# One transformer layer on one core: seven-product blocks for two more projections, cross weights folded elsewhere, pools laid out anew

## The chip, the cores and the metric

The kernel runs on one core of a Trainium2 chip. A core has TensorE for matrix products (PE in the profile; PEld is its loading of the stationary operand), VectorE (DVE), ScalarE (ACT) and GpSimd (POOL) for elementwise work, and a sync engine (SP) whose queue issues this kernel's DMAs. Matrix products go to PSUM, in banks of 128 x 512 floats; all other tiles are in SBUF. The metric is the device time of the whole program in microseconds, as the median of several runs.

## What is computed

One layer of a streaming encoder on 2048 tokens of width 1024, all in float32. Cut to what matters:

```
u = rms_norm(h, g_mix_pre)
z = u @ w_in                                   # 1024 x 2816
qa, ka, va, qh, fh, ih, gh = split(z)          # 512,128,128,512,512,512,512
ya = swa_with_sinks(qa, ka, va, sinks)         # 8 heads of 64, window of 128 tokens
yh = hgrn2(qh, fh, ih, gh, lb, onorm)          # gated recurrence, 4 heads of 128
y  = concat([ya, yh]) @ w_out                  # 1024 x 1024
h  = h + rms_norm(y, g_mix_post)
u  = rms_norm(h, g_x_pre)
m  = rms_norm(mem, g_mem)                      # 256 memory tokens
h  = h + rms_norm(cross_attention(u, m, wq, wk, wv, wo), g_x_post)
u  = rms_norm(h, g_ffn_pre)
h  = h + rms_norm((silu(u @ w_gate) * (u @ w_up)) @ w_down, g_ffn_post)   # inner 2816
```

## The kernel before

Every float32 product is made of three: each operand is split into a rounded part hi and the remainder lo, and hi*hi, hi*lo and lo*hi are summed in PSUM. `mm3` issues these for the projections, `products` for the later stages. The kernel is written as Python generators; a scheduler of the language then puts the instructions of each engine in an order, by the order in which they were written and by what is ready, so work written later can move forward into gaps if its buffers are free.

**The stages.** (1) `mix` normalises the tokens (`norm_half`, with transposes in `transpose_split`) and multiplies them with 22 column tiles of `w_in`, for the first 1024 tokens (b=0) and then for the second (b=1). `wcols` (L141) loads and splits a column tile; `in_cols` runs 24 matmuls for each half of 512 tokens, applies the gates (`decays` makes the recurrence's cumulative factors), and stores z to memory. (2) Beside the first 13 column groups, `fold_cross` multiplies the fixed memory tokens into the cross-attention weights (qk_d and vo_d). (3) `swa` and `hgrn` run attention and recurrence for 16 tiles of 128 tokens, between the column tiles; the last eight steps of the recurrence have nothing written beside them but the loading of `w_out`. (4) `out_proj` makes 16 rows of the output projection, 48 matmuls each, then the norm (`post_norm`), the residual, and the transposed result h1t_d. (5) `phases` runs the rest, scores, values, hidden layer and down projection, in blocks of 256 x 1024 x 1024.

**The blocks.** A block is either of kind "s", seven products of half-size operands (`seven`, a Strassen-like scheme; 84 matmuls of 512 columns for 1024 deep) or of kind "p", the usual eight (`eight`; 96 matmuls). The operand that stays for many blocks ("resident") is held as tiles T, numbered 1 to 8: 1, 8, 2, 3 are its quarters, 5, 7, 6, 4 are sums and differences, built by `resident` from raw halves. "p" needs 1, 2, 8, 3; "s" needs 1, 5, 6, 3, 7, 2, 4. There are seven slots, four of kind A in pool `big`, three of kind B in pool `tb`. The other operand is streamed: `streamed` loads raw tiles (three buffers) and makes S tiles (five buffers) by `split2`, which rounds hi on ACT ("A") or POOL ("P") and subtracts for lo on VectorE. Products accumulate in banks g and t (two each); h and s serve transposes and the small work. `after` of a block (norms, stores, transposes) is run beside the next block. At a change of the resident, the last block and the first are of kind "p", so that fewer tiles are needed while slots change hands.

**Space.** `mix` and `out_proj` hold pools `wp` (weight columns) and `io` (rows) on the right side of SBUF through both; pools xp, ap and later tb lie on the left. So the output projection may begin while the recurrence still runs.

Of the kernel before, what the change touches and what calls it, by code (L numbers as in the profile page):

```python
# [26 lines left out]
NB = 2  # L27
# [13 lines left out]
class Layer:  # L41
# [15 lines left out]
    def xr_tile(self):  # L57
        self._n += 1
        return self.ph.tile([P, D], F32, tag="xr", name=f"xr_{self._n}", bufs=2)

# [52 lines left out]
    def post_norm(self, banks, g, res, dst, t):  # L113
        nc = self.nc
        ss = self.small("p_s", 2)
        for q in range(2):
            nc.scalar.activation(t[:, q * 512:(q + 1) * 512], banks[q], AF.Square, accum_out=ss[:, q:q + 1])
        r = self.rstd([ss[:, 0:1], ss[:, 1:2]], D, "p")
        for q in range(2):
            sl = slice(q * 512, (q + 1) * 512)  # L120
            nc.vector.scalar_tensor_tensor(t[:, sl], banks[q], r, g[:, sl], ALU.mult, ALU.mult)
        nc.gpsimd.tensor_tensor(t, t, res, ALU.add)
        self.store(dst, t)

# [33 lines left out]
    def mm3_pair(self, banks, pairs):  # L158

        nc = self.nc  # L160
        n = len(pairs)
        for i, ((ah, al), (bh, bl)) in enumerate(pairs):
            for q in range(2):
                sl = slice(q * 512, (q + 1) * 512)
                nc.tensor.matmul(banks[q], ah, bh[:, sl], start=(i == 0), stop=False)
                nc.tensor.matmul(banks[q], ah, bl[:, sl], start=False, stop=False)
                nc.tensor.matmul(banks[q], al, bh[:, sl], start=False, stop=(i == n - 1))


    def run(self):  # L170
# [5 lines left out]
        self.y_d = tc.dram_tile([NT, P, KT, P], F32, name="y_d")  # L176
# [9 lines left out]
        with (  # L186
            tc.tile_pool(name="cst", bufs=1) as self.cst,
            tc.tile_pool(name="sm", bufs=3, **kw) as self.sm,
            tc.tile_pool(name="ps", bufs=2, space=PS, **kw) as self.psum,
        ):  # L190
            self.consts()
            with (
                tc.tile_pool(name="gp", bufs=2, **kw) as self.gp,
                tc.tile_pool(name="big", bufs=4, **kw) as self.big,
                contextlib.ExitStack() as self.wp_io,
            ):
                self.wp = self.wp_io.enter_context(tc.tile_pool(name="wp", bufs=3, side="right", **kw))
                self.io = self.wp_io.enter_context(tc.tile_pool(name="io", bufs=2, side="right", **kw))
                wt = self.mix()
                with tc.tile_pool(name="tb", bufs=3, **kw) as self.tb:  # L200
                    self.rows(wt)

    def mix(self):
        tc, I = self.tc, self.I
        kw = dict(reuse_waits="tile")
        us = [[] for _ in range(NB)]
        wt = []

        def norm(b, s, xs=None):
            xs = xs or self.norm_loads(I["x"], b, s, "xxxx" if b else "xxxs")  # L210
            hi, lo = [self.big.tile([P, KT, 512], F32R, tag="big", name=f"u{i}{b}_{s}") for i in "hl"]
            self.norm_half(xs, self.g_mix, us[b], hi, lo, "sh")

        def nxt(b, s):
            if b + 1 < NB:
                norm(b + 1, s)
            else:
                self.out_weights(s, wt)

        with tc.tile_pool(name="mc", bufs=1, **kw) as self.mc:  # L220
            with tc.tile_pool(name="xp", bufs=1, **kw) as self.ph:
                self.g_mix = self.gain(I["g_mix_pre"])
                xs = self.norm_loads(I["x"], 0, 0, "xxxs")
                norm(0, 0, xs)
                norm(0, 1)
                self.mix_consts()
                cols = self.in_proj(0, us[0], lambda: nxt(0, 0))
                side = self.fold_cross()
                for i in range(13):
                    next(cols)  # L230
                    for _ in range(2 if i % 3 else 4):
                        next(side, None)
                for _ in side:
                    pass
            with tc.tile_pool(name="ap", bufs=1, **kw) as self.ph:
# [3 lines left out]
                next(swa)  # L239
                for _ in cols:  # L240
                    pass
                nxt(0, 1)
                cols = self.in_proj(1, us[1], lambda: nxt(1, 0))
                for _ in swa:
                    next(hgrn)
                for _ in hgrn:
                    pass
                for i in range(5):
                    next(cols)
# [5 lines left out]
                nxt(1, 1)  # L255
                for _ in self.hgrn(range(NPB, NT), "hs"):
                    pass
        return wt
# [9 lines left out]
    def fold_cross(self):  # L268

        nc, ph = self.nc, self.ph  # L270
# [5 lines left out]
        kT = [ph.tile([P, KT, M], F32R, name=f"kT{i}") for i in range(2)]  # L276
        vT = [ph.tile([P, KT, M], F32R, name=f"vT{i}") for i in range(2)]

        def split_tiles():
            self._n += 1  # L280
            return [ph.tile([P, D], F32R, tag=t, name=f"{t}_{self._n}", bufs=2) for t in ("xh", "xl")]

        for t in range(M // P):
            m = self.xr_tile()
# [4 lines left out]
        for w, dst in ((self.I["wk_x"], kT), (self.I["wv_x"], vT)):  # L289
            for j in range(KT):  # L290
                raw = self.xr_tile()
                self.load(raw.rearrange("p (k c) -> p k c", k=KT),
                          w[:, j * P:(j + 1) * P].rearrange("(k p) c -> p k c", p=P))
                wh, wl = split_tiles()
                self.split(raw, wh, wl)
                ps = self.bank("sh"[j % 2])[:, :M]
                self.mm3(ps, [((wh[:, k * P:(k + 1) * P], wl[:, k * P:(k + 1) * P]), (mT[0][:, k, :], mT[1][:, k, :]))
                              for k in range(KT)])
                nc.scalar.activation(dst[0][:, j, :], ps, AF.Copy)
                nc.vector.tensor_tensor(dst[1][:, j, :], ps, f32(dst[0][:, j, :]), ALU.subtract)  # L300
                yield
        for d in range(KT):
            wq = self.xr_tile()
# [15 lines left out]
            yield  # L319
        for h in range(4):  # L320
            banks = [[self.bank(k) for k in "sh"] for _ in range(2)]
            for i in range(2):
                j = 2 * h + i
                raw = self.xr_tile()
# [21 lines left out]
    def mix_consts(self):  # L346
# [24 lines left out]
        self.wmask = ph.tile([P, M], F32, name="wmask")  # L371
# [3 lines left out]

        self.reset = ph.tile([P, 8, 64], F32, name="reset")
        nc.vector.memset(self.reset, 1.0)
        nc.vector.memset(self.reset[:, :, 0:1], 0.0)
# [7 lines left out]

        self.dl = ph.tile([P, 4, T // 64 + 1], F32, name="dl")
        nc.vector.memset(self.dl[:, :, 0:1], 0.0)
        self.G = ph.tile([P, NT, 4, 2], F32, name="G")
        self.G1 = ph.tile([P, NT, 4], F32, name="G1")  # L390

    def zero_tiles(self):
        nc, ph = self.nc, self.ph
# [10 lines left out]
    def norm_loads(self, src, b, s, tiles="xxxx"):  # L404

        xs = []
        for t in range(4):
            x = self.xr_tile() if tiles[t] == "s" else self.io_tile("x")
            r0 = b * TB + s * 512 + t * P
            self.load(x, src[r0:r0 + P, :])  # L410
            xs.append(x)
        return xs

    def norm_half(self, xs, g, u, hi, lo, kinds):

        for t, x in enumerate(xs):
            n = self.pre_norm(x, g, True)
            o = t * P
            self.transpose_split(n, lambda q: hi[:, 4 * q:4 * q + 4, o:o + P],
                                 lambda q: lo[:, 4 * q:4 * q + 4, o:o + P], kinds)  # L420
        u.append((hi, lo))

    def in_proj(self, b, u, mid):
        order = [4, 5, 0, 1, 2, 3]
        for h in range(4):
            order += [10 + h, 6 + h]
        order += range(14, 22)
        e1 = None
        for cols in [order[:2]] + [[c] for c in order[2:-2]]:
            e1 = self.in_cols(b, u, cols, e1)  # L430
            yield
        self.in_cols(b, u, order[-2:], None, mid)

    def in_cols(self, b, u, cols, e1, mid=None):
        nc = self.nc
        w = []
        for c in cols:
            first = (b, c) == (0, C_KA // P)
            w.append(self.wcols(self.I["w_in"], c * P, nc.gpsimd if first else nc.vector))
        z = [self.io_tile("z") for _ in cols]  # L440
        for s in range(TB // 512):
            sl = slice(s * 512, (s + 1) * 512)
            if s and mid is not None:
                mid()
# [825 lines left out]
```

## Time and profile before

| | us |
|---|---|
| three runs | 2714.88, 2715.77, 2715.68 (median 2715.68) |
| profiled execution, its own time | 2707.81 |
| its span, first to last instruction | 2706.1 |
| mean granted TensorE clock | 0.992 |

| stage, as the timeline shows it | from about (us) |
|---|---|
| norms, input projection with the folding beside | 0 |
| attention and recurrence with the rest of the projection | 390 |
| last recurrence steps, output projection begins | 770 |
| output projection alone | 870 |
| scores | 1020 |
| values | 1220 |
| hidden layer | 1410 |
| down projection | 2380 |

In a row of the profile, "psg<-uh,whi 128*128 128x512 f32 x704 | 283.1, 403" reads: written tile, then the moving and the stationary operand, their shapes, the count, the busy microseconds and the mean nanoseconds of one. Buffer numbers are left out. What stands behind the second bar is the time in which the engine idled just before, and what ended it.

### The profile page before, as it was taken

What the parts mean: (1) busy time and instruction counts of PE and PEld (TensorE: products, weight loads), DVE (VectorE), ACT (ScalarE), POOL (GpSimd) and SP (SyncE); (2) the same over time, 40 slices, a digit from 0 to 9 for tenths busy, and PEclk for the clock granted to TensorE, in tenths of its full rate; (3) what the DMA queues carried; (4) which work ended last, traced back from release to release, by engine and by line L of the source; (5) the groups of instructions that cost most, each with busy time, mean ns of one, the idle gap of its engine ahead of it and who ended that gap; (6) DMA issues with size and microseconds to landing.
All of it is one profiled execution on the core that took longest, in us unless ns stands there. A gap on an engine that the chain in (4) does not pass through costs nothing.

```text
span 2706.1 us, 34685 instructions
## 1 busy us (share of the span) xinstructions
PE 2626.3 (97%) x12530; PEld 2186.9 (81%) x12530; DVE 1630.8 (60%) x2520; ACT 1002.3 (37%) x2144; POOL 772.2 (29%) x960
## 2 busy tenths in 40 slices
PE   7999999999999998999979999999999999999997
PEld 6888788888887887887768888888888888888776
DVE  5324447769653327677776555566555556576865
ACT  3124335656523334555553222232222233321322
POOL 4213413433164543125651111111111111111255
PEclk9999999999999999999999999999999999999999
DMA  6436546446366745474682222362222244685853
GB/s 197 138 125 211 178 138 174 148 127 190 105 201 214 224 145 174 120 251 155 218 296 93 78 79 86 98 239 76 86 91 82 78 164 157 240 289 198 278 187 125
DMA packets 362220, 436.53 MB, mean 161 GB/s; under 512 B 18369, under 2 KB 276417, under 8 KB 362049
## 3 DMA queue, kind: packets, MB, share of 16 engines
q1 hardware_dynamic: 362048, 434.32, 49.6%
q8 instruction: 99, 1.62, 0.3%
q14 instruction: 73, 0.59, 0.1%
HBM read 304.23 MB, written 130.02 MB: 160 GB/s over the span
## 4 chain that ended last, share of the span: by engine, by line
PE 79%; DVE 6%; POOL 5%; DMA 5%; issue 2%; ACT 2%; SPq 0%; POOLq 0%; DVEq 0%; ACTq 0%
PE psg L856 9%; PE psg L858 9%; PE psg L857 9%; PE pst L856 7%; PE pst L857 7%; PE pst L858 7%; PE psg L154 6%; PE psg L155 6%; PE psg L156 6%; POOL row L1248 1%; PE pst L155 1%; PE pst L154 1%; PE pst L156 1%; DVE S L775 1%; POOL row L1157 1%
## 5 line engine op out<-in xcount | busy, mean ns | idle before, releaser
L856 PE MATMUL psg<-T,S 128*128 128x512 f32 x1312 | 514.2, 393 | 18.0 <-ACT row L1182 6.2
L858 PE MATMUL psg<-T,S 128*128 128x512 f32 x1312 | 512.0, 391 | 1.2 <-DVE S L775 1.2
L857 PE MATMUL psg<-T,S 128*128 128x512 f32 x1312 | 511.8, 390 | 0.0
L856 PE MATMUL pst<-T,S 128*128 128x512 f32 x1034 | 404.6, 392 | 11.4 <-DVE part L873 7.2
L857 PE MATMUL pst<-T,S 128*128 128x512 f32 x1034 | 404.0, 391 | 0.0
L858 PE MATMUL pst<-T,S 128*128 128x512 f32 x1034 | 396.9, 391 | 0.0
L775 DVE TENSOR_TENSOR S<-sraw,S 128x512 fp32r<-128x512 f32 (+1 forms) x265 | 201.3, 769 | 195.5 <-ACT S L772 152.8
L774 POOL TENSOR_SCALAR S<-sum 128x512 fp32r<-128x512 f32 (+1 forms) x142 | 109.2, 769 | 724.0 <-PE psg L858 416.5
L856 PEld LDWEIGHTS psg<-T,S 128*128 128x128 f32 x1312 | 247.3, 189 | 73.2 <-DVE row L1149 7.2
L858 PEld LDWEIGHTS psg<-T,S 128*128 128x128 f32 x1312 | 247.2, 188 | 53.0 <-DVE S L775 1.6
L857 PEld LDWEIGHTS psg<-T,S 128*128 128x128 f32 x1312 | 247.4, 189 | 50.4
L154 PE MATMUL psg<-uh,whi 128*128 128x512 f32 x704 | 283.1, 403 | 1.9 <-ACT uh L110 1.4
L155 PE MATMUL psg<-ul,whi 128*128 128x512 f32 x704 | 282.4, 401 | 0.3 <-DVE ul L111 0.3
L156 PE MATMUL psg<-uh,wlo 128*128 128x512 f32 x704 | 282.2, 401 | 0.0
L856 PEld LDWEIGHTS pst<-T,S 128*128 128x128 f32 x1034 | 195.1, 189 | 53.7 <-DVE part L873 8.5
L858 PEld LDWEIGHTS pst<-T,S 128*128 128x128 f32 x1034 | 195.0, 189 | 40.7 <-DVE S L775 0.4
L857 PEld LDWEIGHTS pst<-T,S 128*128 128x128 f32 x1034 | 195.1, 189 | 40.3
L775 DVE TENSOR_TENSOR S<-sum,S 128x512 fp32r<-128x512 f32 (+1 forms) x284 | 192.3, 686 | 41.9 <-POOL S L774 37.2
L774 POOL TENSOR_SCALAR S<-sraw 128x512 fp32r<-128x512 f32 (+1 forms) x110 | 90.4, 824 | 369.5 <-PE pst L858 162.8
L772 ACT ACTIVATE S<-sum 128x512 fp32r<-128x512 f32 (+1 forms) x142 | 83.4, 616 | 298.8 <-PE psg L858 261.4
L772 ACT ACTIVATE S<-sraw 128x512 fp32r<-128x512 f32 (+1 forms) x155 | 95.7, 617 | 188.4 <-PE psg L858 149.5
L139 DVE TENSOR_TENSOR wlo<-raw,whi 128x1024 fp32r<-128x1024 f32 x59 | 74.8, 1267 | 149.3 <-POOL whi L138 141.8
(346 smaller groups left out, 4634.1 us busy)
## 6 DMA issues: line engine op xcount, KB each, us to landing
row<-in_w_down_dram SPq DMA_DIRECT2D x53, 512.0 KB, 6.1
raw<-in_w_in_dram SPq DMA_DIRECT2D x44, 512.0 KB, 4.3
z_d<-z SPq DMA_DIRECT2D x44, 512.0 KB, 3.4
sraw<-in_w_gate_dram SPq DMA_DIRECT2D x44, 512.0 KB, 3.9
row<-u_d SPq DMA_DIRECT2D x44, 512.0 KB, 7.4
sraw<-in_w_up_dram SPq DMA_DIRECT2D x44, 512.0 KB, 3.8
hid_d<-row SPq DMA_DIRECT2D x44, 512.0 KB, 2.6
row<-h_d SPq DMA_DIRECT2D x32, 512.0 KB, 5.5
```

What stands on the lines that cost most here:

```text
L139: (lo_engine or nc.vector).tensor_tensor(lo, raw, f32(hi), ALU.subtract)
L154: nc.tensor.matmul(ps, ah, bh, start=(i == 0), stop=False)
L155: nc.tensor.matmul(ps, ah, bl, start=False, stop=False)
L156: nc.tensor.matmul(ps, al, bh, start=False, stop=(i == n - 1))
L772: self.nc.scalar.activation(hi, raw, AF.Copy)
L774: self.nc.gpsimd.tensor_scalar(hi, raw, 1.0, 1.0, ALU.mult, ALU.mult)
L775: self.nc.vector.tensor_tensor(lo, raw, f32(hi), ALU.subtract)
L856: nc.tensor.matmul(ps, s[:, 0, k, :], t[:, 0, k, :], start=st, stop=False, **kw)
L857: nc.tensor.matmul(ps, s[:, 0, k, :], t[:, 1, k, :], start=False, stop=False, **kw)
L858: nc.tensor.matmul(ps, s[:, 1, k, :], t[:, 0, k, :], start=False, stop=sp, **kw)
L1157: nc.gpsimd.tensor_tensor(y[i], y[i], x[i], ALU.add)
L1248: nc.gpsimd.tensor_tensor(y[:, sl], y[:, sl], x[:, sl], ALU.add)
```

## The change

The input projection of the first 1024 tokens and the output projection become jobs of `phases`. In the first, the tokens are the resident operand (its quarters made while the norm runs) and two column tiles of `w_in` form a block; eleven blocks, the first two of kind "p". The second half's tokens are normalised beside these blocks, stored transposed to memory (un_d) and fetched back at the end; their projection (`in_proj(1)`) still uses `mm3`, with hi and lo now in one tile. In the second, `w_out` is resident and 256 tokens form a block; eight blocks, the first two and the last of kind "p". `fold_cross` moves beside the last half of the recurrence. The recurrence stores y transposed by tokens. Pools: `ts` (raw and S) is split off `tb`; `wp` and `io` lie on the left and only while the second half runs; the stream pool `t3` opens on the right when the recurrence's pool closes; `gp` has one buffer. The query's scale of -0.125 is applied in `swa_front` instead of at eviction.

```
     def mix(self):
...
+            self.mc = pool("mc", left)
+            with (
+                tc.tile_pool(name="t1", bufs=3, **kw) as self.tb,
+                tc.tile_pool(name="t2", bufs=3, **kw) as self.ts,
+                tc.tile_pool(name="s1", bufs=2, side="right", **kw) as self.st_pool,
+            ):
+                u = self.in_first()
+            self.wp = pool("wp", left)
+            self.io = pool("io", left)
+            self.hg = pool("hg", right, side="right")
+            with tc.tile_pool(name="sw", bufs=1, side="right", **kw) as self.sw:
...
+                cols = self.in_proj(1, u)
+                for _ in range(2):
+                    next(cols)
                 for _ in swa:
                     next(hgrn)
+                    next(cols)
...
+            phases = self.phases(self.jobs(), None, lambda: self.io_tile("z"))
+            with tc.tile_pool(name="xp", bufs=1, side="right", **kw) as self.xp:
+                fold = self.fold_cross()
+                for _ in self.hgrn(range(NPB, NT), "gt"):
+                    for _ in range(2):
+                        next(fold)
+                for _ in range(8):
+                    next(phases)
+                for _ in fold:
                     pass
+            right.close()
+            with tc.tile_pool(name="t3", bufs=3, side="right", **kw) as self.ts:
+                left.close()
+                with (
+                    tc.tile_pool(name="t4", bufs=3, **kw) as self.tb,
+                    tc.tile_pool(name="s3", bufs=2, side="right", **kw) as self.st_pool,
+                ):
+                    for _ in phases:
+                        pass
...
+    def pair_tile(self):
+        self._n += 1
+        return self.st_pool.tile([P, 2, D], F32, tag="pair", name=f"pair_{self._n}", bufs=5)
...
+    def in_first(self):
...
+        def norm(s):
...
+            for i in range(4):
+                x = stage[s][:, i, :]
+                self.normed(x, junk[:, i, :])
+                o = slice(i * P, (i + 1) * P)
+                for q in range(2):
+                    ps = self.bank("sh"[q])
...
+                    t = T[key[q, s]]
+                    nc.scalar.activation(raw[q, s][:, :, o], ps.rearrange("p (j t) -> p j t", j=4), AF.Copy)
+                    self.split2(raw[q, s][:, :, o], t[:, 0, :, o], t[:, 1, :, o], "P")
...
+        beside = [(), (0,), (1, 2), (3,), (4,), (5,), (6,), (7,), (), (), ()]
+        get = fetch()
+        blocks = [("p" if i < 2 else "s",) + self.in_block(*p, beside[i], get if i > 9 else ())
+                  for i, p in enumerate(self.ORDER)]
...
+                t = self.big.tile([P, 2, 4, 512], F32R, tag="big", name=f"u1_{q}{s}")
+                r = second[q, s]
+                for k in (0, 2):
+                    self.split2(r[:, k:k + 2], t[:, 0, k:k + 2], t[:, 1, k:k + 2], "A")
...
+    def in_block(self, ca, cb, beside, get):
...
+        def after():
+            for n, p in x:
+                t, u = p[:, 0, :], p[:, 1, :]
+                self.normed(t, u)
+                yield
+                self.store_transposed(self.un_d, n, self.transposed(t, u))
+            c0 = ca * P
+            if C_FH <= c0 < C_IH:
+                e = self.pair_tile()
+                self.decays(0, (c0 - C_FH) // P, z[0][:, 0, :], e[:, 0, :], e[:, 1, :])
...
     def phases(self, jobs, first, prologue=None):
...
-        queue = sorted(uses, key=lambda k: (uses[k][0] - (4 if k[1] == 7 else 0), k))
+        queue = sorted(uses, key=lambda k: (uses[k][0] - (5 if k[1] == 7 else 0), k))
...
+        def kinds(blocks, n=1):
+            return [("p" if i < n or i == len(blocks) - 1 else "s",) + b for i, b in enumerate(blocks)]
+
+        jobs = [(w_out, 4, kinds([self.mixed_block(n) for n in range(0, NT, 2)], 2)),
+                (weights(self.qk_d, 0, 4), 4, kinds([self.score_block(n) for n in range(0, NT, 2)])),
...
+    def mixed_block(self, n):
...
+        def after():
+            for i in range(2):
+                r = self.rstd(self.square_sum(y[i], "p"), D, "p")
+                nc.vector.scalar_tensor_tensor(y[i], y[i], r, self.g_mix_post, ALU.mult, ALU.mult)
+                nc.gpsimd.tensor_tensor(y[i], y[i], x[i], ALU.add)
+                self.store(self.h1_d[(n + i) * P:(n + i + 1) * P, :], y[i])
+                yield
+                r = self.rstd(self.square_sum(y[i], "n"), D, "p")
+                nc.gpsimd.tensor_scalar(self.r_x[:, n + i:n + i + 1], r, 1.0, None, ALU.mult)
+                yield
+                self.store_transposed(self.h1t_d, n + i, self.transposed(y[i], x[i]))
```

More of the change, by code (lines that the diff above doesn't have):

```diff
@@ L205, in mix, with pool @@
         kw = dict(reuse_waits="tile")
[L206 to L235, printed above, removed]
+        with contextlib.ExitStack() as left, contextlib.ExitStack() as right:
+            def pool(name, at, **k):
+                return at.enter_context(tc.tile_pool(name=name, bufs=1, **k, **kw))
+            self.mc = pool("mc", left)
+            self.r_x = self.cst.tile([P, NT], F32, name="r_x")
+            with (
[8 more added lines that the diff above has]
+            with tc.tile_pool(name="sw", bufs=1, side="right", **kw) as self.sw:
                 self.zero_tiles()
@@ L288, in fold_cross @@
                                  lambda q: mT[1][:, 4 * q:4 * q + 4, t * P:(t + 1) * P])
[L289 to L301, printed above, removed]
+        for kT in projected(self.I["wk_x"]):
+            yield
         for d in range(KT):
-            wq = self.xr_tile()
+            wq = raw_tile()
             self.load(wq, self.I["wq_x"][d * P:(d + 1) * P, :])
@@ L955, in half @@
                 T[k] = dst
[L956 removed]
+                current[:] = [self.resident(fetch(n, tile), jobs[n][1], p, dst, keep[n]), 0]
             next(current[0])
@@ L1060, in rows @@
         jobs[-1][2][-1] = ("s", s, o, f, a)
[L1062 to L1077 removed]
+        return jobs
     def row_tile(self):
```

390 lines of the change are left out of this document (203 added, 187 removed).

## The prediction

> **What bounds the kernel now.** I read the page's engine lines first, then the busy time by windows, then the order of time on TensorE inside one stage of each kind, then what the engines beside it do where TensorE idles.
>
> ```profile
> span 2706.1 us, 34685 instructions
> ...
> PE 2626.3 (97%) x12530; PEld 2186.9 (81%) x12530; DVE 1630.8 (60%) x2520; ACT 1002.3 (37%) x2144; POOL 772.2 (29%) x960
> ...
> PE 79%; DVE 6%; POOL 5%; DMA 5%; issue 2%; ACT 2%; SPq 0%; POOLq 0%; DVEq 0%; ACTq 0%
> ...
> L154 PE MATMUL psg<-uh,whi 128*128 128x512 f32 x704 | 283.1, 403 | 1.9 <-ACT uh L110 1.4
> ```
>
> TensorE (PE) has work almost all the time, and it is 79% of the chain that ended last. A change pays through fewer matmuls, and loses through new places where TensorE waits. A busy time of 403 ns is not the price of a matmul, since the next one starts before it ends; the price is the spacing of starts. The first pair of lines is the input projection, the second pair seven-product work:
>
> ```profile
> 99.74 0.40 PE L154 MATMUL psg<-uh,whi 128*128 128x512 f32 x1
> ...
> 102.55 0.40 PE L154 MATMUL psg<-uh,whi 128*128 128x512 f32 x1
> ...
> 1602.05 0.39 PE L856 MATMUL psg<-T,S 128*128 128x512 f32 x1
> ...
> 1603.87 0.39 PE L858 MATMUL psg<-T,S 128*128 128x512 f32 x1
> ```
>
> Twelve spacings lie between the first two starts: 2.81/12 = 0.234 us each. Eight lie between the last two: 1.82/8 = 0.2275 us. The output projection's own rows (845.58 to 846.52 in the same view) give 0.235 as well.
>
> Windows tell where TensorE idles; columns are start:end, length, then busy us and instructions of PE, PEld, DVE, ACT, POOL, then clock, DMA share, GB/s:
>
> ```profile
> 0.00:25.00 25.00, 11.38 (x40) 8.70 (x41) 14.97 (x26) 13.41 (x23) 13.78 (x21) 1.00 0.95 281
> ...
> 390.00:770.00 380.00, 379.18 (x2064) 321.95 (x2064) 283.47 (x666) 209.81 (x598) 129.12 (x182) 1.00 0.50 150
> 770.00:870.00 100.00, 92.44 (x550) 80.97 (x549) 37.44 (x54) 31.68 (x118) 55.38 (x69) 0.95 0.64 198
> 870.00:1020.00 150.00, 150.00 (x698) 122.64 (x697) 46.36 (x48) 52.27 (x111) 76.32 (x104) 1.00 0.61 199
> 1020.00:1060.00 40.00, 31.56 (x141) 25.09 (x140) 31.56 (x45) 19.16 (x36) 13.05 (x7) 0.96 0.70 223
> 1220.00:1410.00 190.00, 173.45 (x810) 141.05 (x808) 141.19 (x142) 101.74 (x229) 121.06 (x136) 0.99 0.66 219
> ```
>
> The start loses 13.6 us (25.00 less 11.38), the last recurrence half 7.6, the output projection nothing, the change to the scores 8.4, and the value stage, made of seven-product blocks followed by a norm, 16.5.
>
> **The matmuls.** First half of the input projection: 22 column tiles x 2 token halves x 8 x 3 = 1056 matmuls before. After: eleven blocks, two of eight products (96) and nine of seven (84), 948. Output projection: 16 x 2 x 8 x 3 = 768 before; after, three blocks of 96 and five of 84, 708. The new ones are issued by `products` on T and S tiles, so I price them at 0.2275: 1056 x 0.234 - 948 x 0.2275 = 31.4, and 768 x 0.234 - 708 x 0.2275 = 18.6. The gain is **50 us**. If the spacing stays 0.234 it is 168 x 0.234 = 39 us. If the second half's matmuls shorten too, because hi and lo now lie in one tile, 1056 x 0.007 = 7 more, 57. I take 50, because lines 856 to 858 keep their spacing through every later stage. The Trainium skill (TensorE: Matmul & The Clock Gate, "Back-to-back issue gap") gives one isolated spacing at N=512, about 216 ns, whatever code issues it; both rows here are above it and differ, so the trace does not bear out a single figure, but by that rule only the count would pay, 39 us.
>
> **The start (+8, bounds +2 to +16).** Before, ACT rounds hi straight out of PSUM and VectorE subtracts. After, ACT copies to a raw tile and POOL rounds it (`split2` with "P"). POOL's mean rows are 0.43 (n_v), 0.55 (n_r) and 0.84 for a 128x512 rounding (L774), so 2.7 us for each row tile against 1.0. Four tiles from 8.1 us on end at 19 us at best; with a rounding in the S tiles and the waits below nearer 25, against a first product at 21.1 now. Then four more residents must be built during the first two blocks: T7, T5, T6, T4 are eight halves of 1.21 (subtraction) + 1.27 (L775), 20 us of VectorE, beside 10.6 for four norms (1.28 + 2 x 0.68 each, plus slips) and 14 for S tiles, within some 45 us. The five `pair` buffers hold four raw quarters and one prefetched row, so the first block's output must wait until T5 has freed a quarter. This is nearly covered by the two blocks' own 192 x 0.2275 = 44 us; I take 8 us.
>
> **Blocks (+3, bounds 0 to +8).** A block of 84 takes 19.1 us, 20 with eight transposes. VectorE in a forget/query block: 7 S at 0.74, 4 sums at 0.73, 3 adds at 0.685, two scans at 1.26, 1.25 (L497), 2 x 0.68, 2 x 0.73, a norm of 1.5: 18.2 us. It fits, barely; the window from 390 has VectorE at 75% with TensorE idle for 0.8 us.
>
> **Handover to the second half (+4, bounds 0 to +12).** `wp` lies where the B residents lay, so the first weight columns load only after T7's last product, 5.4 us before the last block ends: load 4.3, two roundings at 1.14, a subtraction 1.27 are 7.9. Two to three us show, and more if VectorE is also making the second half's hi/lo tiles (eight times 1.27).
>
> **Attention beside the second half (+1, bounds -1 to +5).** TensorE has 1056 x 0.234 = 247, attention about 86 and half a recurrence 40; VectorE about 315 of these 373 us (sums of the rows of lines 515 to 688, 139, 461 to 497). Covered as now.
>
> **Recurrence with the cross weights (+4, bounds -7 to +35).** The folding moves from under the input projection to the last half recurrence. It issues 576 matmuls of 256 columns (0.120), 96 of 512 and 80 transposes, about 100 us of TensorE, to the recurrence's 40. Its DMAs move with it: 32 weight loads, two of mem and 16 stores of 512 KB, the eight recurrence tiles' 48 of 256 KB, and eight halves of w_out of 512 KB, 43 MB in 140 us or 307 GB/s. All pass through SP's one queue, and weights have two raw buffers. Each step needs a load and a rounding, (4.3 + 1.1 + 1.3)/2 = 3.4 us at the page's median landing, against 2.9 of matmuls. Output blocks can fill the rest once the space of the recurrence is free. I take 4 more than the 7.6 idle now; all 7.6 may go, and 35 is the price if the queue decides (below).
>
> **Output projection (+10, bounds 0 to +16) and change to the scores (-2, bounds -5 to +2).** The new stage is like the value stage: POOL's add with 2.8 us (L1157), row loads, stores. That one idles 16.5 us, 5.6 of which is its first 30 us, where residents change. The old output projection had none. The boundary with the scores then costs what score to value costs now, some 6 instead of 8.4.
>
> **Sum.** -50 + 8 + 3 + 4 + 1 + 4 + 10 - 2 = **-22 us**. The profiled execution took 2707.8 us with a span of 2706.1; the median shown is 2715.7, 7.9 above it. So 2686 for such an execution and **2694 us** for the median. The `gain` tiles with one buffer cost nothing: each next load comes a stage after the last use (hidden under that stage's matmuls; without, one load of 4.7 us).
>
> **Rivals.** (1) *The forecast*: 2681 to 2707. (2) *The matmuls pay in full.* The waits are absorbed, as the 0.8 us in the window from 390 suggests, and only 8 of the 28 us remain: 2715.7 - 50 + 8 = 2674. Against it: every stage of blocks followed by a norm idles now.
> (3) *The other side: the recurrence becomes bound by SP's queue.* Place: the folding's steps. The change puts 43 MB there; the window from 770 moved 198 GB/s and that from 1220 had 219. At 219 GB/s, 43 MB take 196 us instead of 140, 56 more, of which blocks of the output projection hide perhaps 10 to 20. With the rest of the sum: -50 + 24 + 38 = +12, 2728. It decides from the point where the stage is longer by 22 us than I have it (140 + 4), thus below about 43 MB/166 us = 259 GB/s without cover. For it: two raw buffers and one queue. Against it: the first window has 281 GB/s.
> (4) *The start is serial on POOL.* These rows show the same rounding at two prices:
>
> ```profile
> 15.06 2.09 POOL L138 TENSOR_SCALAR whi<-raw 128x1024 fp32r<-128x1024 f32 x1
> ...
> 19.55 1.04 POOL L138 TENSOR_SCALAR whi<-raw 128x1024 fp32r<-128x1024 f32 x1
> ```
>
> The first lay beside a VectorE instruction (14.96 for 1.28) on two SBUF operands. If the 16 new roundings double, 16 x 0.84 = 13 us come on top, 2707. The Trainium skill (SBUF — State Buffer, "Who interferes with whom") states that a VectorE instruction with two SBUF inputs and a POOL instruction reading SBUF block each other in full; the new subtraction has two, where the old read PSUM. The trace agrees with 2.09 against 1.04.
>
> **Chances.** (1) 0.44, (2) 0.17, (3) 0.26, (4) 0.13. A change under 0.2% (5.4 us) can't be told from none. (1) and (2) are faster, (3) is slower but for 0.02 that is the same, (4) splits 0.06 faster and 0.07 same: faster 0.67, same 0.09, slower 0.24. The range reaches from below case 2 (2661, 57 us gained and little lost) to above case 3 (2734).
>
> **What would show it.** 948 and 708 matmuls at 856 to 858's successors with 0.227 spacing bear out the first term; the windows give the others: the first 25 us, the stretch around the pool change, the recurrence with its GB/s and the landing of weight loads (now 4.3), the output stage's idle time. I am wrong if the recurrence lasts over 165 us, if VectorE ends most waits within the first eleven blocks, or if the later seven-product stages, which no line changes, have another spacing, now that S tiles lie on the other side of memory.

## The result and the profile after

The kernel after takes 2748.46 us (median of four runs, 2745.87 to 2750.71), the kernel before 2715.28 beside it. The ratio is 1.0126, with a 95% interval of 1.0109 to 1.0144: the change makes the kernel 1.3% slower. The prediction was 2694 us, with a range up to 2734, and so was wrong in the sign and in the range. The profiled execution has a span of 2748.5 us against 2706.1, which is 42 us more.

The engine lines of the page of the kernel after:

```profile
span 2748.5 us, 34989 instructions
...
PE 2641.2 (96%) x12362; PEld 2164.3 (79%) x12362; DVE 1786.9 (65%) x2709; ACT 1095.1 (40%) x2321; POOL 790.2 (29%) x1002
```

There are 168 matmuls fewer (12,530 less 12,362), as counted. Yet TensorE is busy for 14.9 us more, and the rest of the span, in which it idles, has grown from 79.8 us (2706.1 less 2626.3) to 107.3, by 27.5. The second number is what the wait terms of the prediction came to (28). The first was to be -50. So the fault lies in the matmuls themselves.

One stretch is enough to see it. By window, the kernel before (first row) and the kernel after (second row) in 980 us of the hidden layer (in the first row the last 20 us are down projection), stages which no line of the diff touches; columns are start:end, length, busy us and instructions of PE, PEld, DVE, ACT, POOL, granted clock, DMA share, GB/s:

```profile
1420.00:2400.00 980.00, 979.91 (x4323) 811.70 (x4322) 590.16 (x852) 297.56 (x487) 125.38 (x158) 1.00 0.38 125
```

```profile
1420.00:2400.00 980.00, 980.00 (x4175) 787.74 (x4174) 561.20 (x816) 287.41 (x476) 117.04 (x154) 1.00 0.34 113
```

TensorE is full in both, at the full granted clock, and in the same time it gets 148 matmuls fewer through. All its helpers do less, too. The order of time on TensorE shows why; here in the kernel after:

```profile
1601.85 0.39 PE L891 MATMUL psg<-T,S 128*128 128x512 f32 x1
...
1602.78 0.39 PE L892 MATMUL psg<-T,S 128*128 128x512 f32 x1
...
1603.49 0.39 PE L892 MATMUL psg<-T,S 128*128 128x512 f32 x1
```

From the first start to the last are seven spacings: 1.64/7 = 0.234 us. The same loop had 0.2275 before. Over the whole trace, the seven- and eight-product matmuls from the output projection on (7,746) are 0.234 apart, those of the first half of the input projection 0.227. Of the 7,746, 7,038 are in stages that no line changes; their mean spacing, stalls left out, went from 0.2269 to 0.2343: 7,038 x 0.0074 = 52 us.

### The profile page after: what moved, and what is told of

Same layout as the page of the kernel before. It is cut to its first block, busy times and chain, and to the rows that moved or that the text cites. A ratio compares the mean times of both kernels' runs of the same rounds, so it can differ in the third digit from the quotient of the medians.

```text
span 2748.5 us, 34989 instructions
## 1 busy us (share of the span) xinstructions
PE 2641.2 (96%) x12362; PEld 2164.3 (79%) x12362; DVE 1786.9 (65%) x2709; ACT 1095.1 (40%) x2321; POOL 790.2 (29%) x1002
## 4 chain that ended last, share of the span: by engine, by line
PE 74%; DMA 8%; POOL 6%; DVE 6%; issue 3%; ACT 2%; SPq 1%; POOLq 0%; ACTq 0%; DVEq 0%
PE psg L893 11%; PE psg L891 11%; PE psg L892 11%; PE pst L891 9%; PE pst L892 9%; PE pst L893 9%; PE psg L140 2%; PE psg L139 2%; PE psg L138 2%; DMA row<-vo_d 1%; POOL row L1324 1%; DMA qd<-z_d 1%; POOL row L1233 1%; ACT junk L1141 1%; DMA sraw<-hid_d 1%
## 5 line engine op out<-in xcount | busy, mean ns | idle before, releaser
L891 PE MATMUL psg<-T,S 128*128 128x512 f32 x1548 | 620.1, 401 | 28.1 <-ACT row L1258 6.7
L893 PE MATMUL psg<-T,S 128*128 128x512 f32 x1548 | 618.8, 400 | 0.5 <-DVE S L814 0.5
L892 PE MATMUL psg<-T,S 128*128 128x512 f32 x1548 | 617.1, 399 | 0.0
L891 PE MATMUL pst<-T,S 128*128 128x512 f32 x1178 | 467.6, 398 | 6.7 <-DVE part L908 6.6
L892 PE MATMUL pst<-T,S 128*128 128x512 f32 x1178 | 468.3, 398 | 0.0
L893 PE MATMUL pst<-T,S 128*128 128x512 f32 x1178 | 460.5, 398 | 1.4 <-DVE S L814 1.4
L814 DVE TENSOR_TENSOR S<-sraw,S 128x512 fp32r<-128x512 f32 (+1 forms) x327 | 258.1, 800 | 243.6 <-ACT S L811 183.1
L891 PEld LDWEIGHTS psg<-T,S 128*128 128x128 f32 x1548 | 294.8, 190 | 104.6 <-ACT part L906 8.3
L893 PEld LDWEIGHTS psg<-T,S 128*128 128x128 f32 x1548 | 294.3, 190 | 71.4 <-DVE S L814 1.4
L892 PEld LDWEIGHTS psg<-T,S 128*128 128x128 f32 x1548 | 295.1, 191 | 69.9
L891 PEld LDWEIGHTS pst<-T,S 128*128 128x128 f32 x1178 | 222.7, 189 | 61.6 <-DVE part L908 7.9
L814 DVE TENSOR_TENSOR S<-sum,S 128x512 fp32r<-128x512 f32 (+1 forms) x340 | 234.5, 699 | 55.5 <-POOL S L813 43.8
L893 PEld LDWEIGHTS pst<-T,S 128*128 128x128 f32 x1178 | 222.6, 189 | 55.6 <-DVE S L814 2.0
L892 PEld LDWEIGHTS pst<-T,S 128*128 128x128 f32 x1178 | 222.3, 189 | 53.0
L811 ACT ACTIVATE T<-row 128x1024 fp32r<-128x1024 f32 (+1 forms) x134 | 135.7, 1027 | 155.5 <-DVE row L831 31.4
L814 DVE TENSOR_TENSOR T<-row,T 128x1024 fp32r<-128x1024 f32 (+1 forms) x134 | 166.5, 1254 | 47.9 <-ACT T L811 47.7
L906 ACT ACTIVATE part<-psg 128x512 f32<-128x512 f32 x144 | 85.8, 596 | 187.9 <-PE psg L893 178.3
L1141 ACT ACTIVATE junk<-row 128x512 f32<-128x512 f32 x160 | 100.0, 626 | 134.9 <-POOL row L1166 37.5
```

The costliest lines, as they stand in the source:

```text
L811: self.nc.scalar.activation(hi, raw, AF.Copy)
L814: self.nc.vector.tensor_tensor(lo, raw, f32(hi), ALU.subtract)
L891: nc.tensor.matmul(ps, s[:, 0, k, :], t[:, 0, k, :], start=st, stop=False, **kw)
L892: nc.tensor.matmul(ps, s[:, 0, k, :], t[:, 1, k, :], start=False, stop=False, **kw)
L893: nc.tensor.matmul(ps, s[:, 1, k, :], t[:, 0, k, :], start=False, stop=sp, **kw)
L906: nc.scalar.activation(t, ps, AF.Copy)
```

## The experiments

The S tile (stationary) had moved to the right side of memory, the T tile (moving) stayed on the left. The first four runs asked whether that is the cause. Ratios are to the kernel before, run beside them on the same chip (2706.3 us for these four).

**S back on the left.** `e1_s_low` is the kernel after with one word changed in `made`:

```
-            t = self.ts.tile([P, 2, 4, P], F32R, tag="S", name=f"S_{self._n}", bufs=5)[:, :, :nk, :]
+            t = self.tb.tile([P, 2, 4, P], F32R, tag="S", name=f"S_{self._n}", bufs=5)[:, :, :nk, :]
```

> Address theory (a 512-column matmul whose stationary tile lies near the top of SBUF is spaced 0.234 us, else 0.227): with only the S tiles of the later stages moved from the top to 89 to 109 KB, spacing of the block products from 900 us on goes from 0.234 back to 0.227, 7746 matmuls x 0.0075 = 58 us, time about 2690. Rival (the longer spacing comes from something else that changed, such as the order of work or the split of hi and lo): spacing stays 0.234, time 2743 to 2753.

Measured: 2710.40 us, ratio 1.0014 (1.0003 to 1.0025), all spacings of block products 0.227. The place of one tile makes over 1% of the time. The spacing is as the theory asked; the time is 20 us above its 2690.

**A control.** `e2_raw_low` moves the raw tile of `streamed` to the left in the same way and leaves S on the right.

> Control: the same amount of layout change, but the raw tiles go down and S stays at the top (209 to 229 KB). Address theory: spacing stays 0.234 in every later stage, time 2740 to 2756. Rival (any shift of the pools, or where the DMAs land, sets the spacing): spacing 0.227, time about 2690.

Measured: 2752.06 us, ratio 1.0164 (1.0149 to 1.0179), spacing 0.234. It is S, not the room or the traffic around it.

**The sides of the kernel before exchanged.** `e3_before_w_low` puts `big`, `tb` on the right and `wp`, `io`, `st` on the left.

> The kernel before with sides swapped: weight columns of both projections at 36 to 52 KB instead of 205 to 229 KB, the resident tiles (moving operand) at the top instead. Address theory of the stationary operand: spacing of the 2880 projection matmuls goes from 0.234 to 0.227, 20 us less, about 2695; the later stages keep 0.227 though their moving tiles lie at the top. Rival (it is a moving tile at the top, or the distance of the two, that costs): later stages go to 0.234, about 2745. Rival (the projection's code is slower by itself): no change, 2715.

Measured: 2708.35 us, ratio 1.0003 (0.9992 to 1.0015). The later stages keep 0.227 with T and S both high in memory, and the projections keep 0.234 on average (0.231 to 0.237 by line) although their weights now lie low. So a high address is not the cause: that theory falls.

**Matmuls alone, each place in memory.** `e4_map` runs 24 matmuls for each place of the stationary tile, in steps of 4 KB, with the moving tile low and then high.

> Only matmuls, nothing of the layer is computed: 24 of 512 columns for each of 50 places of the stationary tile (every 4 KB from 20 to 225 KB) with the moving tile at 33 KB and again at 213 KB, then 256 columns, then the moving tile at 13 places with the stationary at 62 KB. Address theory: spacing 0.227 below a border between 175 and 205 KB and 0.234 above it, whatever the moving tile's place; 256 columns show 0.120 either way. Rival: no step, or a step with the moving tile's place.

Measured: 0.2267 us for 110 of the 111 series of 512 columns that follow the first, 0.2279 for the other. Neither the place nor the side matters by itself. What all its tiles share is that they start a whole multiple of 4 KB apart.

So the next theory was about the distance of the two tiles' starts, modulo some small number. I first took 64 bytes, as the pools on the two sides start 32 apart in that measure.

**Shifted by 32 bytes.** `e5_after_pad` and `e6_before_pad` make one constant of 128x8 floats 128x16 in either kernel, which shifts the whole left side by 32 bytes:

```
-        self.mhalf = self.cst.tile([P, 8], F32, name="mhalf")
+        self.mhalf = self.cst.tile([P, 16], F32, name="mhalf")
```

> The kernel after with one constant tile 32 bytes wider, so that every pool on the left side of memory starts 32 bytes further; the pools on the right stay where they are. Phase theory: the 512-column matmuls of the output projection and of the six later stages were 7.5 ns apart longer because their S tile (right side) and their T tile (left side) start 32 bytes apart modulo 64; now both agree, all 7,746 of those matmuls run at 0.227 us, the time falls by about 55 us against the kernel after, to some 2690 (2683 to 2700), below the kernel before. In the second half of the input projection and in the cross weights whi and the tiles of the folding change their phase too; they may lose or gain 5 us. Rival, that the S tile's distance from T, its side, or the traffic of the DMAs beside it sets the spacing: 0.234 stays and the time stays within 5 us of 2748.

> The kernel before with the same edit. Phase theory: the later stages have S and T both on the left, both move, and stay at 0.227 us; the projections have the weights on the right and the tokens on the left, which differ by 32 bytes modulo 64 in the kernel before and agree now, so their 2,880 matmuls go from 0.234 to 0.227 and the time falls by 15 to 22 us, to some 2695. Rival: nothing changes, 2713 to 2717.

Measured: 2737.53 us, ratio 1.0110 (1.0093 to 1.0127), spacing 0.233; and 2705.98 us, ratio 0.9993 (0.9984 to 1.0002), projections still 0.233. Both miss: 64 bytes is the wrong period.

**A map by offsets.** `e7_phase_map`:

> Matmuls alone, 24 after each other for each pair of offsets: the stationary block starts 0, 2, 4 ... 32 elements into its tile, the moving block 0, 4, 8 or 16 elements into its own; then the same with 256 and 128 columns. It leaves out the whole computation of the reference. Phase theory: the spacing depends on the difference of the two offsets modulo 16 elements (64 bytes), 0.227 us where it is nothing and 0.234 where it is 8 elements. Rival, that the phase is not the cause: 0.227 throughout.

Measured: 0.227 to 0.228 with both blocks at offset 0, both at 32 bytes, or both at 64; 0.233 with one of them 32 bytes further than the other; with 64 bytes, 0.233 where the stationary block lies further and 0.229 where the moving one does. Some pairs at 8- and 16-byte offsets are fast as well, and one with both at 16 bytes is not (0.231), which no rule of mine explains. With 256 columns the spacing is 0.113 to 0.120, with 128 it is 0.112, without such a pattern. So the distance matters, and 64 bytes (0.233) don't restore it.

**Shifted by 96 bytes, and a finer map.** By the address table of the compiled programs, T and S start 119,904 or 185,440 bytes apart in the kernel after, 96 more than a multiple of 512; in the kernel before, T and S are exact multiples apart, while its projections' tokens and weights are again 185,440 apart. `e8_after_pad96` and `e9_before_pad96` have `[P, 32]` in the line above, 96 bytes more.

> The kernel after with one constant tile 96 bytes wider instead of 32, so that the left side of memory starts 96 bytes further. In all fast groups so far the stationary and the moving tile start a whole multiple of 512 bytes apart (126,976, 61,440, 65,536, 20,480, 77,312 and 16,384 bytes), in all slow ones 64, 96 or 416 bytes more than a multiple (185,440 and 119,904 in the kernel after, 185,408 and 119,872 with 32 bytes of padding). Pitch theory: now every pair is 0 modulo 512 apart, the 7,746 matmuls from the output projection on run at 0.227 us, and the time falls by some 50 to 60 us against the kernel after, to 2680 to 2700, under the kernel before. Rival, that the side of the S tile sets the spacing and not the distance: 0.234 stays, 2737 to 2750.

> The kernel before with the same edit: the distance of the projections' weights from their tokens becomes 185,344 bytes, 362 times 512. Pitch theory: the projections' 2,880 matmuls go from 0.234 to 0.227 us, later stages stay at 0.227, the time falls by 15 to 22 us to some 2690. Rival, that matmuls in threes on one pair of banks are slower whatever the addresses: no change, 2705 to 2712.

> Matmuls of 512 columns alone, 24 after each other for each stationary start of 0 to 1,056 bytes in steps of 32 into a tile, at moving starts of 0, 64 and 96 bytes, then the first row again in descending order. It leaves out the whole computation of the reference. Pitch theory: 0.227 us where the two starts are the same or some fixed power of two apart, 256 or 512 bytes as may be, and 0.230 to 0.235 at most others; the same value both ways through the list. Rival, that the spacing depends on what ran before: the two passes differ.

Measured: the kernel after with 96 bytes takes 2701.58 us, ratio 0.9983 (0.9975 to 0.9992); the kernel before with them 2697.24, ratio 0.9963 (0.9951 to 0.9975), with its projections at 0.227 in the median (0.227 to 0.230 in the mean of a line) and a gain of 10 us by the ratio, where I had expected 15 to 22; TensorE's busy time fell by 11.2. The map, mean spacing in ns over 24 matmuls by the stationary block's start less the moving block's:

```
bytes    0   32   64   96  128  160  192  224  256  288  ...  448  480  512  768  1024
ns     227  233  233  234  233  233  229  233  227  233  ...  229  233  227  227   227
```

The same row comes out with the moving block 64 or 96 bytes into its tile, and, to within 2 ns, in descending order. For tiles that start at multiples of 32 bytes the period is **256 bytes**: 226.7 ns at a multiple of it, 229 at 64 bytes less, 233 to 234 at the other steps of 32. Every group of the kernels fits, with 96 bytes over in the kernel after (0.234), 64 with the 32-byte padding (0.233), 0 with the 96-byte one. The hidden layer with 96 bytes:

```profile
1420.00:2400.00 980.00, 979.95 (x4323) 811.45 (x4322) 590.89 (x853) 296.42 (x486) 124.29 (x158) 1.00 0.36 126
```

4,323 matmuls again. Padding alone gives the kernel after 1.0126 - 0.9983 = 1.4%, 39 us of 2708 (46 between the profiled spans); by the two intervals 1.2 to 1.7%. I had expected 50 to 60: the busy time fell by 54.5 us, and 8.2 of it turned into waits.

**What is left.** With the distance mended in both, the change is still not faster: 2701.58 against 2697.24. The engine lines of those two, the kernel before (first) and after (second), both with 96 bytes:

```profile
span 2694.1 us, 34685 instructions
...
PE 2615.1 (97%) x12530; PEld 2186.1 (81%) x12530; DVE 1632.9 (61%) x2520; ACT 1002.5 (37%) x2144; POOL 770.5 (29%) x960
```

```profile
span 2702.2 us, 34989 instructions
...
PE 2586.7 (96%) x12362; PEld 2160.4 (80%) x12362; DVE 1779.4 (66%) x2709; ACT 1094.1 (40%) x2321; POOL 794.9 (29%) x1002
```

The matmuls pay 28.4 us and the idle time takes 36.5 (115.5 less 79.0). VectorE has 146 us more work. Four more runs ask where, all with 96 bytes.

**A third buffer for raw weights.** `e11_raw3` changes `bufs=2` to `bufs=3` in `raw_tile`.

> The kernel with 96 bytes of padding, and a third buffer for the raw weight tiles of the projections and the folding. If the recurrence stage is held by the latency of loads that are issued when a buffer comes free, the waits of POOL for raw tiles (18 us in 650 to 780) go and the time falls by 5 to 15 us against the version with padding alone. If SP's queue or the DMA bandwidth holds it (my third rival: more loads in flight don't help, their time only grows), less than 3 us, either sign.

Measured: 2696.08 us, ratio 0.9963 (0.9951 to 0.9976), 5.5 us less than without. TensorE's busy time in 650 to 780 rises from 119.3 to 121.3 us of 130, so only part of the gain lies in that stage. POOL's waits for raw weights there, 18.7 us without the third buffer, are gone. The gain is at the low end of what latency would give and above what a queue at its limit would; the intervals touch (0.9975), so the size is loose.

**No seven-product blocks in the input projection.** `e13_in_plain` makes all of them eight products:

```
-        blocks = [("p" if i < 2 else "s",) + self.in_block(*p, beside[i], get if i > 9 else ())
+        blocks = [("p",) + self.in_block(*p, beside[i], get if i > 9 else ())
```

> The same version (2696) with all eleven blocks of the first half of the input projection in eight products: 108 matmuls more, 24.5 us at 0.227 us. If the matmul count is what that stage is paid by, 20 to 25 us slower, about 2718. If its other engines (VectorE above all, with the sums of seven products) hold it, the waits of 100 to 300 (16 us) go in exchange and the price is 8 to 15 us.

Measured: 2698.60 us, ratio 0.9966 (0.9954 to 0.9978): within the uncertainty of the version it is made from. 108 matmuls more cost nothing that shows. By window, the version with seven products (first) and with eight:

```profile
100.00:200.00 100.00, 92.80 (x411) 76.32 (x410) 69.36 (x89) 58.41 (x92) 40.12 (x47) 0.95 0.44 132
200.00:280.00 80.00, 76.40 (x333) 62.03 (x333) 48.75 (x69) 25.75 (x42) 12.49 (x16) 1.00 0.57 181
280.00:320.00 40.00, 36.09 (x172) 29.63 (x171) 12.50 (x38) 9.76 (x32) 11.08 (x15) 1.00 0.66 171
```

```profile
100.00:200.00 100.00, 100.00 (x463) 83.29 (x462) 33.62 (x40) 37.20 (x54) 34.50 (x39) 1.00 0.38 116
200.00:280.00 80.00, 79.40 (x358) 65.22 (x357) 27.91 (x33) 25.91 (x40) 12.69 (x18) 1.00 0.53 173
280.00:320.00 40.00, 40.00 (x188) 33.52 (x189) 16.31 (x48) 11.12 (x33) 13.81 (x20) 1.00 0.77 215
```

VectorE's work in 100 to 200 halves (69.36 to 33.62), ACT's and POOL's falls too, and TensorE hardly idles, at the handover to the second half either (the last row). Over the whole run TensorE is busy for 19.7 us more and idles for 17.2 less, 14.1 of it in 25 to 300. So the work that seven-product blocks add costs about what they save; which of the three engines holds TensorE, this run does not tell.

**More plain blocks in the output projection.** `e12_out3` and `e14_out_plain` change the 2 in `kinds(..., 2)` of the first job to 3 and to 8.

> The version with 96 bytes of padding and three raw buffers (2696 when the kernel before took 2706), and the third block of the output projection in eight products too, not in seven: 12 matmuls more, 2.7 us if nothing else changes. If the 12 us that TensorE idles around 850 to 900 come from the loads of the three residents that only seven-product blocks use, with the x rows queued among them, the later need gives time back and it ends 2 to 9 us earlier; if the stall only moves on to the fourth block, it ends 0 to 3 us later.

> The same version (2696) with all eight blocks of the output projection in eight products: 60 matmuls more, 13.6 us. If seven products pay there, 8 to 14 us slower; if their residents' loads and sums cost as much as the matmuls they save, within 4 us of 2696.

Measured: 2704.45 us, ratio 0.9991 (0.9982 to 1.0000), for three plain blocks at the start, a loss of 8, and 2695.21, ratio 0.9956 (0.9944 to 0.9968), for all eight, no difference that can be told. The first misses both expectations: the stall does not shrink but moves on and adds to itself (TensorE busy for 38.1 us in 850 to 900 and 94.8 in 900 to 1000, against 42.8 and 98.8 in the version it is made from); why it grows stays open. With all eight plain, the stage is full from 850 on, but a wait of 8.9 us stands ahead of it. The version with seven products (first) and with eight:

```profile
780.00:850.00 70.00, 66.34 (x324) 55.61 (x323) 29.14 (x30) 16.71 (x32) 18.00 (x17) 1.00 0.69 217
850.00:900.00 50.00, 42.77 (x177) 34.23 (x178) 39.86 (x39) 29.30 (x63) 31.86 (x37) 0.86 0.74 226
900.00:1000.00 100.00, 98.82 (x474) 82.09 (x473) 65.86 (x67) 58.03 (x132) 66.63 (x89) 1.00 0.74 243
```

```profile
780.00:850.00 70.00, 61.08 (x293) 51.36 (x293) 28.91 (x27) 22.87 (x43) 19.45 (x20) 0.93 0.68 235
850.00:900.00 50.00, 50.00 (x239) 41.71 (x238) 14.44 (x14) 23.21 (x59) 30.70 (x47) 1.00 0.55 182
900.00:1000.00 100.00, 100.00 (x480) 83.58 (x479) 36.83 (x33) 46.67 (x108) 54.68 (x80) 1.00 0.64 204
```

TensorE idles for 12.1 us of these 220 with seven products and for 8.9 with eight.

The last version, with 96 bytes, a third buffer and a plain output projection, beats both kernels: 0.44% under the kernel before, 1.7% under the kernel after. It does not beat the kernel before with its own padding (0.9963) by anything that can be told.

## Why the prediction was wrong

**Matmuls (-50).** This term is the wrong one, by 65 us of busy time. The count was right. The step that failed is "I take 50, because lines 856 to 858 keep their spacing through every later stage": I tied the spacing to the code that issues the matmuls, and it belongs to the distance of two tiles in memory, modulo 256 bytes. So the 7,038 matmuls of unchanged stages went from 0.227 to 0.234 (+52 us), and the output projection kept its 0.234 (+5). The second half's matmuls, at 0.229 instead of 0.234, give 5 back, which the sum had left out. Some 13 of the 65 us remain. By the clock records of the two traces, TensorE was busy at half the clock for 15 to 23 us longer (the first 27 us of the kernel before have no record), which costs half of that, 7 to 11; the rest stays open. With the distance mended (`e8_after_pad96`) the busy time is 39.6 us under that of the kernel before, still not 50, with the same time at half the clock. The condition stood in the list of what would prove me wrong, but with no price and no place in the range. It would have been easy to give it one from the rows shown: all those matmuls at the projections' spacing. The row that I read as two kinds of code (uh,whi at 0.234; T,S at 0.2275) was two distances: padding took the projections of the kernel before to 0.227 with no line of their code changed. The Trainium skill (TensorE: Matmul & The Clock Gate, "Back-to-back issue gap") makes the isolated spacing depend on the column count alone, about 216 ns at N=512. That the code does not matter holds here; that the columns alone decide does not, with 226.7 to 234 ns for the same 512, and no series of the maps has a mean under 226.7.

**Waits (+28).** Their sum was right for the change as it ran (27.5 us more idle time), but by luck. By the windows of the two traces, TensorE idles for 69.6 us up to and with the change to the scores, where it was 32.5, so 37 more; behind that, where no line differs, for 37.7 against 47.3, 10 less. While the matmuls were 3% slower, the other engines had that much more time, which would explain the 10; no run separates it. With the distance mended in both kernels the difference is 36.5. Then the change brings 3.9 us between the profiled spans (2702.2 against 2706.1 of the kernel before) in place of 22: about 10 are missing in busy time and 8 in waits.

**Start (+8) and blocks (+3).** The first product starts at 25.13 us, "nearer 25" as put down, against 21.09 before. The first 25 us of the kernel after:

```profile
0.00:25.00 25.00, 6.69 (x32) 5.47 (x32) 15.77 (x19) 14.80 (x26) 16.35 (x26) 0.87 0.98 298
```

TensorE idles for 18.3 us in them, where it was 13.6: 5 us, not 8. The waits that end in 25 to 300, what waits and for what, total, times, longest:

```profile
PE psg L891 <- POOL u L813: 7.6, 1, 7.6
PE psg L891 <- ACT part L906: 4.0, 3, 3.0
PE pss L1076 <- DVE pair L378: 3.1, 1, 3.1
PE psg L140 <- DVE wlo L123: 2.1, 2, 1.1
```

POOL's rounding ends the longest, which is the one just ahead of the first product. That is not rival 4, though: the 16 roundings did not double but took 16.2 us, 1.03 each against the 0.84 in the sum, 3 us in place of 13. The blocks were taken too cheaply: TensorE idles for 12.6 us in 25 to 290, where it was 1.6. "It fits, barely" compared 18.2 us of VectorE's work with a block's 20, which leaves 2 us for VectorE's own waits. In 25 to 280 of the kernel after, VectorE's group for the S tiles of raw halves shows what such waits are (after the second bar the idle time before them and what ended it):

```profile
L814 DVE TENSOR_TENSOR S<-sraw,S 128x512 fp32r<-128x512 f32 x31 | 24.5, 806 | 22.0 <-ACT S L811 13.5 <-POOL S L813 8.4
```

22 us of waiting for ACT's and POOL's roundings stand beside 24.5 us of work, and what is queued behind them on VectorE waits too. The plain version puts the price of the seven products here, blocks and handover together, at 17.2 us of waits, where I had 3 + 4.

**Recurrence (+4, bounds -7 to +35).** The price of rival 3, with SP's queue as the bound, did not come. By window in the kernel after:

```profile
650.00:720.00 70.00, 60.01 (x452) 57.38 (x451) 40.91 (x55) 29.16 (x80) 30.52 (x33) 0.95 0.81 222
720.00:780.00 60.00, 56.58 (x472) 55.74 (x471) 25.75 (x40) 25.55 (x75) 18.56 (x21) 1.00 0.81 253
```

The recurrence lasts from some 655 to 771, under 120 us; the last part of the folding runs on to 838 beside the first output blocks. The two together take longer than the 166 us at which the rival would decide, but TensorE is kept busy meanwhile: it idles 13.4 us in these windows and 2.3 in 780 to 850, where the last recurrence half had 7.6, so the term is 6 to 8. That a third raw buffer helped speaks for latency. And 253 GB/s is not the most that this queue moved, since the first 25 us have 298.

**Output projection (+10).** The waits do not spread over the stage as in the value stage. All 11.5 us lie in 850 to 900, at the first seven-product block, whose residents' halves and token rows are loaded all at once when the folding's space comes free. The chain of waits of the kernel after:

```profile
846.70 10.40 DMA row<-in_x_dram
857.11 8.84 DMA row<-in_w_out_dram
866.07 1.23 DVE row L828
```

The rows land after 10.4 us, behind them the sums wait, and TensorE's transposes wait for POOL's addition to the same rows (8.1 us of the waits). With all blocks plain the busy time of the run grows by 8.7 us and the idle time falls by 8.3, of which 3.2 lie in 780 to 1000; 2.8 lie in 25 to 300, which the edit does not touch, so these differences are loose by some 3 us. A wait for `w_out` remains, earlier. The size, 10, was about right; what I did not see is that the seven products would bring nothing to set against it.

So the change won nothing that can be told in the two stages where it takes matmuls away: 168 matmuls are worth 38 us at 0.227, but taking them out lowered TensorE's busy time by only 28.4 us (19.7 and 8.7) and brought 25.5 us of waits (17.2 and 8.3), before the tiles' distance costs 39 more. Of the missing 10 us, some 7 are matmuls at half the clock by the records of these traces: 60.8 us of busy time in the version with seven products, 51.5 and 56.5 in the two plain ones.

## What to carry to other kernels

When pools move, work out the distance of the stationary and the moving tile of each matmul loop modulo 256 bytes, and pad one small tile until it is 0 (with starts at multiples of 32 bytes, as the map had them); here 96 bytes were worth 39 us in one kernel and 10 in the other. The spacing of matmul starts in a stage that the diff does not touch is the first row to compare. And a product less per block pays only where the engines that make its sums and roundings keep up: in the hidden layer VectorE was busy for 60% and TensorE full, in 25 to 280 of the kernel after for 70%, and TensorE waited. Cost their queues with the waits in them, not the sum of the work for one block.

## What was not expected of the hardware

The distance of the operands: 226.7 ns at multiples of 256 bytes, 229 at 64 less, 233 at other steps of 32, for fp32r matmuls of 512 columns with a weight load each. Why it is so, no run here tests.

After a stall the matmuls themselves are slower. In 862 to 880 of the kernel after, groups on TensorE by line (count, busy us, mean ns of one, idle time before):

```profile
L891 PE MATMUL psg<-T,S 128*128 128x512 f32 x7 | 4.0, 576 | 0.7 <-ACT row L1160 0.7
...
L1076 PE MATMUL pss<-ident,row 128*128 128x128 f32 x4 | 1.1, 435 | 4.4 <-POOL row L1166 4.4
```

576 ns, where the mean of this line over the kernel is 401, in a stretch with a mean granted clock of 0.73 (by the records, half speed to 865.0 and from 871.8 to 878.6). A wait of some microseconds thus costs more than its idle time. The Trainium skill (TensorE: Matmul & The Clock Gate, "What's actually happening") has it that the throttled state is the default, which activity releases. The trace fits: 0.73 in these 18 us, with the waits in them, and 1.00 from 900 on, where TensorE is full.
